# Second layer's MLP: 24 f tiles of M1 as seven half-size products per four tiles, M2's weight sums by accumulating transfers

## The chip, the cores and the metric

The kernel runs on one core of a Trainium2 chip. A core has five engines with instruction streams of their own: TensorE (PE; its weight loads are shown as PEld), VectorE (DVE), ScalarE (ACT), GpSimd (POOL) and SyncE (SP, which issues most transfers), and 16 DMA engines that move data between device memory and the on-chip memory. The metric is the device time of one execution in microseconds, and of several runs the median. The profile is one execution taken by the hardware profiler; its times are microseconds from the start of its span.

## The reference

A decoder of two layers on 512 tokens with D = 1024 and D_FF = 4096, in float32, cut to what matters here:

```
c_act = silu(c)
for i in range(2):
    sh1, sc1, g1, sh2, sc2, g2 = split(c_act @ ada_w[i] + ada_b[i], 6)
    h = rmsnorm(x, norm_mix_g[i]) * (1 + sc1) + sh1
    y = pool_mixer(h) if i == 0 else sgu_mixer(h)
    x = x + g1 * y
    h = rmsnorm(x, norm_mlp_g[i]) * (1 + sc2) + sh2
    x = x + g2 * (square(relu(h @ mlp_w1[i])) @ mlp_w2[i])
return rmsnorm(x, final_g)
```

`sgu_mixer` is a projection to 2048 columns with GELU, a layernorm of one half (v), a causal 128 x 128 mixing per head, a product with the other half (u) and a last projection, called M_o below. `mlp_w1` (1024 x 4096) is M1, `mlp_w2` (4096 x 1024) is M2.

## The kernel before

**Precision.** Each float32 operand of a large product is kept as two parts: hi, a rounded copy written by ScalarE, and lo, the difference written by VectorE (`split`, lines 135 to 140, for weights). A product is then three matmuls, lo x hi, hi x lo and hi x hi (`mm3`, lines 145 to 149). The partition size P is 128, KD = 8 tiles of D, NT = 4 tiles of tokens, S = 512 tokens. `hh` and `hl` hold the two parts of the normalised, transposed input.

**The MLP of a layer** is `mlp(i, first, extra, last, ending)` at line 506. M1 makes 32 f tiles of 128 columns each. An f tile takes eight steps over D, of three matmuls with 512 columns (`f_run`, line 544), and `put` (522) writes relu and then the square into `g` with ScalarE (532, 533). Eight f tiles form a chunk. M2 takes chunk 0, 1 and 2 as a 2 x 2 block product with seven half-size products instead of eight (`p_prep` 565, `p_run` 610, numbered 1, 5, 6, 3, 7, 2, 4 in the order in which they run; the pattern is that of Strassen and Winograd). Their operands are sums of blocks: VectorE adds blocks of M2's weights, 128 x 2048 each, in place (574, 580, 591, 599), and blocks of g (576, 582, 584, 588). The result is accumulated into `y` (632, 635), and in chunk 2 multiplied by the gate `gb` and added to x (the fold, 638 and 639). The last chunk is taken directly (`q_prep` 644, `q_run` 666), and the callback `last` finishes x.

**Order.** PE's instructions run in the order in which the program gives them. For the other engines a list scheduler sets the order, by priority and by when buffers come free. The units of the MLP (f tiles, products p, last products q) are listed in lines 678 to 689: after the first f tiles three f tiles of the next chunk, and from then on p and f in turn. Unit n + 2 is prepared (loaded and split) before unit n runs (694 to 697). Loads of weights use the pool `w4` (three buffers of 128 x 1024, shared with several smaller users), the split weights five pairs of buffers `wh`, `wl`, and blocks of M2 three buffers `b` of 1 MB.

**Extras.** Work for later that is spread over the units (698 to 700). In the second layer these are eight `ada_tile` (162; a load into a w4 buffer and a multiply-and-sum on VectorE), which make the last columns g2 of the modulation, then `spread_cols` (176), which spreads these columns over all partitions: eight GpSimd operations fill `dg` (line 180, a w4 buffer), two matmuls with a matrix of ones put it into PSUM (183), and ScalarE copies that into `gb` (184). The tenth extra, `load_fg` (873), loads the final norm's gain.

**Start of the second MLP.** In the M_o stage (838 to 853) `gated` (706) adds the mixer's result to x and collects the norm's sums; `power` on GpSimd (190) makes the inverse root. `normed(hf, ...)` (725) scales x, transposes it on PE (737) for one half of the tokens (256), applies the modulation into a tile `tt`, and makes hi and lo (745, 746). `first1` (855) runs f tiles 0 to 3 in two halves of 256 tokens: the first half of tiles 0, 1 and 2, then `normed` for the second half of the tokens, the first half of tile 3, and the second halves of the four.

The modulation's loads, the loads of x, M1 and M2 are issued on SP's queue.

Of the kernel before, what the change touches and what calls it, by code (L numbers as in the profile page):

```python
# [70 lines left out]
def decoder_kernel(ctx: ExitStack, tc: tile.TileContext, xtok, vecs, rows, fgrow, ada0, adag, ada1, pool_w, w1s, w1, w2, w2e, w_v, w_u, w_o, wsT, lnp, bs, out):  # L71
# [40 lines left out]
    x = big.tile([P, NT, D], F32, name="x")  # L112
    hh = big.tile([P, KD, S], F32R, name="hh")
    hl = big.tile([P, KD, S], F32R, name="hl")
    gb = big.tile([P, D], F32, name="gb")

# [83 lines left out]
    with (  # L200
# [29 lines left out]
        def squares(out, t, c, on):  # L230
            j = sq[:, 0 : c.stop - c.start]
            if on is A:
                A.activation(j, x[:, t, c], AF.Square, scale=D**-0.5, accum_out=out)
            else:
                V.scalar_tensor_tensor(j, x[:, t, c], 1.0 / D, x[:, t, c], ALU.mult, ALU.mult, accum_out=out)
# [39 lines left out]
        def load(name):  # L275
# [8 lines left out]
            if kind == "x":  # L284
                for t in range(NT):
                    nc.sync.dma_start(x[:, t], xtok[t])
            elif kind == "pw":
                c = slice(2 * d[0], 2 * d[0] + 2)
                nc.sync.dma_start(pw[:, c], pool_w[:, c])
            elif kind == "raw":  # L290
                sweep_load(d[0])
# [73 lines left out]
        def windows(g):  # L365

            for k in (2 * g, 2 * g + 1):
                po = pqs[k] = bank("pq")
                for t in range(NT):
                    n = P if t == NT - 1 else W  # L370
                    T.matmul(po[:, P * t : P * t + n], x[:, t, P * k : P * k + P], bandr[:, t, g, 0:n], start=(t == 0), stop=(t == NT - 1), skip_group_check=True)
# [18 lines left out]
        def add(g, h):  # L390
            c = slice(256 * g, 256 * g + 256)
            V.tensor_tensor(x[:, 2 * h : 2 * h + 2, c], x[:, 2 * h : 2 * h + 2, c], pos.pop((g, h)), ALU.add)  # L392
# [6 lines left out]
        def turn(g):  # L399

            for k in (2 * g, 2 * g + 1):
                pxs[k] = bank("px")
                for t in range(NT):
                    T.transpose(pxs[k][:, P * t : P * t + P], x[:, t, P * k : P * k + P], ident)
# [57 lines left out]
        def norm_hi(k):  # L462
            t = ht[k] = st2.tile([P, S], F32, name="ht", tag="ht")
            V.scalar_tensor_tensor(t, xf[:, k], scl[0][1][:, k : k + 1], rbs[0], ALU.mult, ALU.mult)
            A.activation(hh[:, k], t, AF.Identity, bias=mod(0, c_sh(1, k)))  # L465

        def norm_lo(k):
            V.scalar_tensor_tensor(hl[:, k], ht.pop(k), mod(0, c_sh(1, k)), f32(hh[:, k]), ALU.add, ALU.subtract)
# [22 lines left out]
        for k in range(KD):  # L491
# [11 lines left out]
            for f in range(SWEEP):  # L503
                mm3(sweep[f], cut(wk[k][1:], ALL, slice(P * f, P * f + P)), (hh[:, k], hl[:, k]), k == 0, k == KD - 1)


    def mlp(i, first, extra, last, ending):
# [3 lines left out]
        with (  # L511
# [6 lines left out]
            tc.tile_pool(name="yp", bufs=1) as yp,  # L518
# [3 lines left out]
            y = yp.tile([P, NT, D], F32, name="y")  # L522
            g = {}

            def put(f, po):
# [3 lines left out]
                if p == 0:  # L529
                    g[c, j] = gq.tile([P, 4, S], F32, name="g", tag="g")  # L530
                t = g[c, j][:, p]
                A.activation(t, po, AF.Relu)  # L532
                A.activation(t, t, AF.Square)  # L533
# [6 lines left out]
            def f_prep(u):  # L540
                c, f = u
                return split(raw4(w1[i, 8 * c + f]))

            def f_run(u, w):
# [3 lines left out]
                for k in range(KD):  # L548
                    mm3(po, cut(wv, ALL, k), (hh[:, k], hl[:, k]), k == 0, k == KD - 1)
# [3 lines left out]

            held = {}

            def b_of(c, r, n):
                t = w2p.tile([P, 4, S], F32, name="b", tag="b")
                nc.sync.dma_start(t, w2[i, c, r, n])
                return t

            def p_prep(u):
                c, m = u
                H = held
# [4 lines left out]
                if m == 1:  # L568
                    wb = H["b11"] = b_of(c, 0, 0)
                    a = quad(c, 0, 0)  # L570
                elif m == 5:
                    H["b12"] = b_of(c, 0, 1)
                    wb = H["t"] = H.pop("b11")
                    V.tensor_tensor(wb, H["b12"], wb, ALU.subtract)
                    a = H["s"] = s_tile("s")
                    V.tensor_tensor(a, quad(c, 1, 0), quad(c, 1, 1), ALU.add)
                elif m == 6:
                    H["b22"] = b_of(c, 1, 1)
                    wb = H["t"]
                    V.tensor_tensor(wb, H["b22"], wb, ALU.subtract)  # L580
                    a = H["s"]
                    V.tensor_tensor(a, a, quad(c, 0, 0), ALU.subtract)
                    H["u"] = s_tile("u")
                    V.tensor_tensor(H["u"], quad(c, 0, 0), quad(c, 1, 0), ALU.subtract)
                elif m == 3:
                    wb = H["b22"]
                    a = H["s"]
                    V.tensor_tensor(a, quad(c, 0, 1), a, ALU.subtract)
                elif m == 7:
                    wb = H.pop("b12")  # L590
                    V.tensor_tensor(wb, H.pop("b22"), wb, ALU.subtract)
                    a = H.pop("u")
                    H.pop("s")
                elif m == 2:
                    wb = H["b21"] = b_of(c, 1, 0)
                    a = quad(c, 0, 1)
                else:
                    wb = H.pop("t")
                    V.tensor_tensor(wb, H.pop("b21"), wb, ALU.subtract)
# [3 lines left out]
                A.activation(oh, a, AF.Copy)  # L603
                V.tensor_tensor(ol, a, f32(oh), ALU.subtract)
                w = [split(wb[:, 2 * q : 2 * q + 2].rearrange("p a b -> p (a b)")) for q in range(2)]
                return (oh, ol), w

            X, Z = {}, {}
# [4 lines left out]

            def p_run(u, ready):
# [3 lines left out]
                banks = X if m in (1, 6, 7, 4) else Z  # L618
                first, fin = m in (1, 5, 2), m in (4, 3, 2)
                if first:  # L620
                    for hf in halves:
                        banks[hf] = bank("pm", xz)
                for p in range(4):
                    wv = cut(w[p // 2], ALL, slice(S * (p % 2), S * (p % 2) + S))
                    for hf in halves:
                        mm3(banks[hf], cut(o, ALL, p, hf), wv, first and p == 0, fin and p == 3, skip_group_check=True)
                for hf in halves:
                    r, dh = TAKES[m]
                    t = 2 * hf + r
                    yt = y[:, t, S * dh : S * dh + S]  # L630
                    if (t, dh) in seen:
                        V.tensor_tensor(yt, yt, banks[hf], ALU.add)  # L632
                    else:
                        seen.add((t, dh))
                        A.activation(yt, banks[hf], AF.Copy)
                    if c == 2 and LAST.get(m) == (r, dh):

                        V.tensor_tensor(yt, yt, gb[:, S * dh : S * dh + S], ALU.mult)
                        V.tensor_tensor(x[:, t, S * dh : S * dh + S], x[:, t, S * dh : S * dh + S], yt, ALU.add)
# [4 lines left out]
            def q_prep(u):  # L644
# [8 lines left out]
                else:  # L653
                    o = w2p.tile([P, 2, KD, P], F32R, name="qo", tag="b")
                    oh, ol = o[:, 0], o[:, 1]
                for j in range(2):
                    a, k = g[3, j][:, :, tok[t]], slice(4 * j, 4 * j + 4)
                    A.activation(oh[:, k], a, AF.Copy)
                    V.tensor_tensor(ol[:, k], a, f32(oh[:, k]), ALU.subtract)
# [3 lines left out]
            kept = {}  # L663

            def q_run(u, o):
                dh, t = u

# [12 lines left out]
            for c in range(3):  # L680
                fs = [("f", (c + 1, f)) for f in range(8)]
                units += fs[0:3]
                fs = fs[3:]
                for m in (1, 5, 6, 3, 7, 2, 4):
                    units.append(("p", (c, m)))
                    if fs:
                        units.append(fs.pop(0))
            units += [("q", (dh, t)) for dh in range(2) for t in range(NT)]
            prep = {"f": f_prep, "p": p_prep, "q": q_prep}
            run = {"f": f_run, "p": p_run, "q": q_run}  # L690
# [3 lines left out]
            for n, (kind, u) in enumerate(units):  # L694
                for m in range(n, min(n + 3, len(units))):
# [5 lines left out]
                run[kind](u, ready[n])  # L701

# [3 lines left out]
    def gated(t, c0, n, src):  # L706
        tmp = sm.tile([P, S], F32, name="tmp", tag="tmp")[:, 0:n]
        xt = x[:, t, c0 : c0 + n]
# [16 lines left out]
    def normed(hf, i, n):  # L725

        xs = []
        for r in range(2):
            t = w4.tile([P, D], F32, name="xs", tag="w4")
            A.activation(t, x[:, 2 * hf + r], AF.Copy, scale=rms(2 * hf + r))  # L730
            xs.append(t)
        c = slice(256 * hf, 256 * hf + 256)
        for k in range(0, KD, 2):
# [4 lines left out]
            tt = sm.tile([P, 2, 256], F32, name="tt", tag="tmp")  # L738
# [240 lines left out]
```

## Time and profile before

| | |
|---|---|
| Median of 3 runs | 895.44 us (895.14 to 895.63) |
| The profiled execution | 895.87 us, of which the span is 894.2 us |
| Mean granted TensorE clock | 0.992 |
| Instructions on PE, DVE, ACT, POOL | 3980, 842, 609, 102 |

A row of a timeline gives the start, the busy time, the engine, the line of the program, the operation, its output and inputs by name and their sizes; in brackets is the engine's idle time just before it and what ended that. A row of a group gives the number of operations, their sum and the mean length in ns. `po`, `pm`, `px`, `pb` are PSUM tiles of the M1-like products, of M2, of the transposes and of `spread_cols`; `raw` is a loaded weight, `wh`, `wl` its two parts, `xs` the scaled x.

### The profile page before, as it was taken

What the parts mean: (1) busy time and instruction counts of PE and PEld (TensorE: products, weight loads), DVE (VectorE), ACT (ScalarE), POOL (GpSimd) and SP (SyncE); (2) the same over time, 40 slices, a digit from 0 to 9 for tenths busy, and PEclk for the clock granted to TensorE, in tenths of its full rate; (3) what the DMA queues carried; (4) which work ended last, traced back from release to release, by engine and by line L of the source; (5) the groups of instructions that cost most, each with busy time, mean ns of one, the idle gap of its engine ahead of it and who ended that gap; (6) DMA issues with size and microseconds to landing.
All of it is one profiled execution on the core that took longest, in us unless ns stands there. A gap on an engine that the chain in (4) does not pass through costs nothing.

```text
span 894.2 us, 10448 instructions
## 1 busy us (share of the span) xinstructions
PE 866.9 (97%) x3980; PEld 719.1 (80%) x3980; DVE 652.0 (73%) x842; ACT 419.8 (47%) x609; POOL 56.2 (6%) x102
## 2 busy tenths in 40 slices
PE   4979999999999999999999999999999999999996
PEld 2868888788888888888878888988887888888885
DVE  5879796779869888746798645657667666667954
ACT  3374755454444445347233336644545445445421
POOL 7000002000000000001310000000003000000000
PEclk9989999999999999999999999999999999999998
DMA  9939853563465442622657206622352134121312
GB/s 356 402 136 325 280 211 130 191 208 118 165 212 164 131 153 71 235 84 105 212 185 239 72 23 235 213 94 89 134 179 94 48 141 144 45 77 65 95 48 94
DMA packets 35475, 138.64 MB, mean 155 GB/s; under 512 B 3937, under 2 KB 4065, under 8 KB 32225
## 3 DMA queue, kind: packets, MB, share of 16 engines
q1 hardware_dynamic: 35282, 137.72, 44.5%
q8 instruction: 31, 0.51, 0.2%
q10 hardware_dynamic: 144, 0.26, 0.1%
q14 instruction: 18, 0.15, 0.0%
HBM read 135.87 MB, written 2.10 MB: 154 GB/s over the span
## 4 chain that ended last, share of the span: by engine, by line
PE 89%; DMA 5%; DVE 3%; ACT 2%; issue 0%; POOL 0%; SPq 0%; POOLq 0%; DVEq 0%; ACTq 0%
PE po L148 18%; PE po L149 18%; PE po L147 17%; PE pm L148 11%; PE pm L149 11%; PE pm L147 11%; DMA ada<-in_ada 1%; DMA wh<-in_adag 1%; DMA wl<-in_ada 1%; PE po L828 1%; DMA wh<-in_ada 1%; PE pb L183 1%; DVE ada L311 1%; DVE x L392 0%; ACT wh L138 0%
## 5 line engine op out<-in xcount | busy, mean ns | idle before, releaser
L147 PE MATMUL po<-hh,wl 128*128 128x512 f32 (+1 forms) x608 | 232.7, 383 | 2.5 <-ACT hh L465 2.4
L148 PE MATMUL po<-hl,wh 128*128 128x512 f32 (+1 forms) x608 | 231.2, 380 | 1.9 <-DVE hl L746 1.7
L149 PE MATMUL po<-hh,wh 128*128 128x512 f32 (+1 forms) x608 | 230.8, 380 | 0.0
L139 DVE TENSOR_TENSOR wl<-b,wh 128x1024 fp32r<-128x1024 f32 x84 | 102.5, 1222 | 70.6 <-ACT wh L138 70.6
L139 DVE TENSOR_TENSOR wl<-raw,wh 128x1024 fp32r<-128x1024 f32 x89 | 108.8, 1223 | 47.2 <-ACT wh L138 46.8
L148 PEld LDWEIGHTS po<-hl,wh 128*128 128x128 f32 x608 | 115.0, 189 | 24.8 <-DVE hl L746 2.1
L147 PEld LDWEIGHTS po<-hh,wl 128*128 128x128 f32 x608 | 115.1, 189 | 24.8 <-ACT hh L465 2.6
L149 PEld LDWEIGHTS po<-hh,wh 128*128 128x128 f32 x608 | 114.9, 189 | 21.4
L149 PE MATMUL pm<-wh,oh 128*128 128x512 f32 x336 | 130.7, 389 | 0.0
L147 PE MATMUL pm<-wh,ol 128*128 128x512 f32 x336 | 130.7, 389 | 0.0
L148 PE MATMUL pm<-wl,oh 128*128 128x512 f32 x336 | 130.7, 389 | 0.0
L138 ACT ACTIVATE wh<-raw 128x1024 fp32r<-128x1024 f32 x89 | 94.1, 1058 | 52.9 <-PE pm L149 34.0
L532 ACT ACTIVATE g<-po 128x512 f32<-128x512 f32 x64 | 38.0, 599 | 170.5 <-PE po L149 170.5
L138 ACT ACTIVATE wh<-b 128x1024 fp32r<-128x1024 f32 x84 | 88.5, 1053 | 15.1 <-PE pm L149 10.1
L169 DVE SCALAR_TENSOR_TENSOR ada<-ada,cb 128x1024 f32<-128x1024 f32 x56 | 68.1, 1219 | 20.0 <-DMA ada<-in_ada 20.0
L147 PEld LDWEIGHTS pm<-wh,ol 128*128 128x128 f32 x336 | 63.1, 188 | 13.1
L148 PEld LDWEIGHTS pm<-wl,oh 128*128 128x128 f32 x336 | 63.1, 188 | 13.1
L149 PEld LDWEIGHTS pm<-wh,oh 128*128 128x128 f32 x336 | 63.1, 188 | 13.1
L714 ACT ACTIVATE tmp<-x 128x512 f32<-128x512 f32 (+1 forms) x25 | 15.3, 613 | 64.5 <-DVE x L710 64.5
L632 DVE TENSOR_TENSOR y<-y,pm 128x512 f32<-128x512 f32 x68 | 43.4, 679 | 0.0
L533 ACT ACTIVATE g<-g 128x512 f32<-128x512 f32 x64 | 39.6, 624 | 0.0
L180 POOL TENSOR_SCALAR dg<-ident,mods 128x128 f32<-128x128 f32 x24 | 24.6, 1044 | 214.3 <-DVE wl L139 129.6
(161 smaller groups left out, 1155.2 us busy)
## 6 DMA issues: line engine op xcount, KB each, us to landing
ada<-in_ada SPq DMA_DIRECT2D x78, 512.0 KB, 4.1
raw<-in_w SPq DMA_DIRECT2D x57, 512.0 KB, 3.4
b<-in_w SPq DMA_DIRECT2D x24, 1024.0 KB, 4.8
raw<-in_w2e SPq DMA_DIRECT2D x16, 512.0 KB, 3.4
ur<-in_w_u SPq DMA_DIRECT2D x8, 512.0 KB, 4.9
raw<-in_w_v SPq DMA_DIRECT2D x8, 512.0 KB, 4.0
raw<-in_w_o SPq DMA_DIRECT2D x8, 512.0 KB, 4.2
wh<-in_ada SPq DMA_DIRECT2D x7, 512.0 KB, 9.8
```

The costliest lines, as they stand in the source:

```text
L138: A.activation(h, r, AF.Copy)
L139: V.tensor_tensor(l, r, f32(h), ALU.subtract)
L147: T.matmul(o, wl, mh, start=first, stop=False, **kw)
L148: T.matmul(o, wh, ml, start=False, stop=False, **kw)
L149: T.matmul(o, wh, mh, start=False, stop=last, **kw)
L169: V.scalar_tensor_tensor(r, r, 1.0, cb, ALU.mult, ALU.mult, accum_out=pmv[i, b][:, j : j + 1])
L180: G.tensor_scalar(dg[:, k], ident, cols[:, k : k + 1], None, ALU.mult)
L183: T.matmul(po, ones, dg[:, 4 * n : 4 * n + 4], start=True, stop=True)
L532: A.activation(t, po, AF.Relu)
L533: A.activation(t, t, AF.Square)
L632: V.tensor_tensor(yt, yt, banks[hf], ALU.add)
L714: A.activation(tmp, xt, AF.Square, scale=D**-0.5, accum_out=s[:, len(cs) : len(cs) + 1])
```

## The change

In the second layer only (the first layer gets the same code with its old shapes, and one sign convention is turned so that VectorE adds blocks of M2's weights where it subtracted them):

- The 24 f tiles of chunks 1 to 3 are made four at a time, as a 2 x 2 block product with seven half-size products (units "s": chunk c, group j of four f tiles, product m). The blocks are halves of D (512 rows), halves of the four f tiles (256 columns) and halves of the tokens (256). A product is eight steps of three matmuls with 256 columns. A block of weights is one 128 x 1024 buffer of w4; VectorE adds blocks in place and splits each sum. Four input sums (operands of products 5, 6, 3 and 7) are made once, from the float32 input `h32`, after f tiles 4 to 7, which run in two halves of 256 tokens now. Products 1, 5 and 6 copy their PSUM into g; 2, 3 and 7 add theirs to g on VectorE; relu and square follow.
- M2's weight sums of chunks 0 to 2 are no longer made by VectorE. GpSimd issues a transfer that adds the next block from device memory to the block in place (`b_add`), once the block's two parts have been made: the running sum `bt` gets the blocks for products 5, 6 and 4, another buffer gets the sum for product 7. There are two buffers `b` and one `bt` where three `b` were.
- x is two tiles of two token tiles each. After each `normed` of the second MLP its half is written to device memory (`spill`), and the space then holds the two parts of the operands of products 6 and 3. After the last product 4 of M1 x is loaded again (`reload`), followed by `load_fg`. The fold of chunks 0 to 2 moves from the p units to the q units.
- `h32` lies in the space of y, and of the mixer's v before that.
- The eight `ada_tile` of the extras move into the M_o stage, one after each `gated`. `spread_cols` is the only extra left, and so is issued with the first unit, before f tile 4 runs.
- A unit's preparation may be up to five weight buffers ahead in place of two units.
- The program is built with 8192 bytes of scratch memory for transfers whose descriptors GpSimd makes.

The core of the diff:

```diff
+            def a_sums(step):
+                def a(r, j):
+                    return h32[0][:, 4 * j : 4 * j + 4, 256 * r : 256 * r + 256]
...
+                if step == 0:
+                    sums_a.update({1: H(slice(0, 4), first), 2: H(slice(4, 8), first), 4: H(slice(4, 8), half)})
+                    shift(hx, GAP)
+                    minus(a(1, 1), a(1, 0), a(1, 1))
+                    m, o = 5, operand(hx, "hx")
+                elif step == 1:
+                    minus(a(1, 1), a(1, 1), a(0, 0))
+                    m, o = 6, operand(big, "x0")
+                elif step == 2:
+                    minus(a(0, 0), a(0, 0), a(1, 0))
+                    V.tensor_tensor(a(1, 1), a(1, 1), a(0, 1), ALU.add)
+                    m, o = 3, operand(big, "x1")
+                else:
+                    m, o = 7, H(slice(0, 4), half)
+                parts(o, a(0, 0) if m == 7 else a(1, 1))
...
+            def s_prep(u):
+                c, j, m = u
...
+                t = b(0, 0)
+                if m in CHAIN:
+                    V.tensor_tensor(t, t, b(*CHAIN[m]), ALU.add)
...
+                elif m == 7:
+                    wb = b(0, 1)
+                    V.tensor_tensor(wb, wb, b(1, 1), ALU.add)
...
+                w = split(wb)
...
+            def s_run(u, w):
...
+                for f in range(2):
+                    for k in range(4):
+                        mm3(po[:, f], cut(wv, ALL, k, slice(P * f, P * f + P)), cut(sums_a[m], ALL, k), start and f + k == 0, stop and f + k == 4, skip_group_check=True)
...
+            def b_add(t, c, r, n):
+                G.dma_start(t, w2[i, c, r, n], accum_op=ALU.add)
...
+                    nxt = {1: 5, 5: 6, 6: 4}.get(m)
+                    if nxt:
+                        b_add(wb, c, *CHAIN[nxt])
+                    if m == 3:
+                        b_add(B["b12"], c, 1, 1)
...
+                    fs, lead, step = [("s", (c + 1, j, m)) for j in range(2) for m in ORDER], 3, (2, 2, 2, 2, 2, 1, 0)
...
+                if i and kind == "f":
+                    a_sums(u[1] - 4)
+                if i and u == (3, 1, 4):
+                    reload()
...
+    def spill(h):
+        xd.append(dram.tile([P, 2, D], F32, name=f"xd{h}"))
+        G.dma_start(xd[h], x_[h])
+
+    def reload():
+        for h in range(2):
+            x_[h] = big.tile([P, 2, D], F32, name=f"x{h}", tag=f"x{h}")
+            G.dma_start(x_[h], xd[h])
+        load_fg()
...
-    ex = [lambda q=q: ada_tile(1, 40 + q, ada1[48 + q], get4) for q in range(8)]
-    ex += [lambda: spread_cols(mods[1][:, c_g(1, 0) : c_g(1, 0) + KD]), load_fg]
+    ex = [lambda: spread_cols(mods[1][:, c_g(1, 0) : c_g(1, 0) + KD])]
```

309 lines of the change are left out of this document (214 added, 95 removed).

## The prediction

> **What bounds the kernel now.** First the page: its span and busy times, then its chain of waits.
>
> ```profile
> span 894.2 us, 10448 instructions
> PE 866.9 (97%) x3980; PEld 719.1 (80%) x3980; DVE 652.0 (73%) x842; ACT 419.8 (47%) x609; POOL 56.2 (6%) x102
> PE 89%; DMA 5%; DVE 3%; ACT 2%; issue 0%; POOL 0%; SPq 0%; POOLq 0%; DVEq 0%; ACTq 0%
> ```
>
> TensorE is busy for 97% of the span and holds 89% of the chain, so time is won only by giving it less to do, and lost wherever it is made to wait. The changed part is the second layer's M1 and M2, from about 537 us on. The windows view (length, then PE, PEld, DVE, ACT, POOL busy, granted clock, DMA share, GB/s) shows it by stage:
>
> ```profile
> 537.00:574.00 37.00, 35.33 (x260) 33.19 (x259) 22.11 (x32) 24.71 (x38) 1.41 (x2) 1.00 0.64 228
> 596.00:664.00 68.00, 68.00 (x302) 56.33 (x301) 48.71 (x46) 35.79 (x46) 0.00 (x0) 1.00 0.35 116
> 664.00:730.00 66.00, 66.00 (x289) 53.94 (x288) 43.97 (x39) 31.87 (x40) 9.79 (x8) 1.00 0.25 88
> ```
>
> From 574 us TensorE never stops; VectorE is at 67 to 72%, ScalarE about half, the DMA engines a third. Before 574 us, where the normalised input is made, it loses about 1.7 us.
>
> **TensorE's work.** A busy matmul's length includes its drain, so I take the price from start to start in the timeline of PE: first the 512-column matmuls, 159 steps from the first to the second row, then the 256-column ones, 51 steps.
>
> ```profile
> 575.01 0.39 PE L147 MATMUL po<-hh,wl 128*128 128x512 f32 x1
> 611.05 0.39 PE L147 MATMUL po<-hh,wl 128*128 128x512 f32 x1
> ...
> 550.38 0.28 PE L149 MATMUL po<-hh,wh 128*128 128x256 f32 x1
> 556.49 0.28 PE L149 MATMUL po<-hh,wh 128*128 128x256 f32 x1
> ```
>
> That is 36.04/159 = 0.2267 us and 6.11/51 = 0.1198 us: half the columns cost 53%, with a new weight load for each. 24 f tiles now take 24 x 24 = 576 long matmuls, 130.6 us. Six groups of seven products, each 2 x 4 x 3 = 24 short matmuls, are 1008, or 120.8 us: **9.8 us less**. The four other f tiles after the first four now run in two halves: 192 short (23.0) for 96 long (21.8), **1.2 us more**.
>
> **The start of the layer.** Rows of the PE timeline, then DVE, then the DMA of the chain and the ScalarE operations behind it:
>
> ```profile
> 538.97 1.91 PE L737 MATMUL px<-ident,xs 128*128 128x128 f32 x16
> 550.15 0.39 PE L148 MATMUL po<-hl,wh 128*128 128x256 f32 x1 [1.31 <-DVE hl L746]
> 564.29 0.39 PE L148 MATMUL po<-hl,wh 128*128 128x256 f32 x1 [0.34 <-DVE hl L746]
> 573.50 0.28 PE L149 MATMUL po<-hh,wh 128*128 128x256 f32 x1
> 573.62 0.40 PE L147 MATMUL po<-hh,wl 128*128 128x512 f32 x1
> ...
> 540.84 3.93 DMA raw<-in_w
> 544.85 1.06 ACT wh L138
> ```
>
> In the built order of the changed kernel ScalarE makes all hi parts of the input (two pairs of tt and two of hh, about 4.2 us at 0.5 us each) before it splits any M1 weights, so both hl stalls should go. But eight ada loads now sit in the M_o stage and hold the w4 buffers; the first M1 weights can only load when the transposes that end near 540.6 release theirs: landing 544.7, ScalarE free at about 545.6, hi 546.7, lo 547.9. f tile 0 starts at 548.0 instead of 546.1. Then 3 tiles (8.6), transposes (1.7), one tile (2.9) and four second halves (11.5) end at 572.6, against 573.6: **1.0 us less**, with 0 and 2 as bounds (all gain eaten by late loads; first load no later than ScalarE's first split today). The eight multiplies of ada move to where VectorE is idle, and cost nothing while M_o runs; if it were late for the mixer's last two tiles, some 4 us of slack is in front of them. The spill of x is issued on POOL's queue ahead of the small power operations (line 190) that the transposes wait for. They have 1 to 3 us of slack.
>
> **A new wait.** spread_cols fills the buffer dg on POOL and multiplies it by ones (line 183) to make gb. It was the ninth extra of the layer, spread over many units; now it is the only one and stands in front of f tile 4 in PE's fixed order. In the built order dg gets the w4 buffer of f tile 7's weights, so POOL starts only after their lo part. The old trace has that subtraction, the three dg fills, pb, and for single fills the shortest, median and longest in ns:
>
> ```profile
> 572.52 1.22 DVE L139 TENSOR_TENSOR wl<-raw,wh 128x1024 fp32r<-128x1024 f32 x1 [1.66 <-ACT wh L138]
> ...
> 144.97 6.48 POOL L180 TENSOR_SCALAR dg<-ident,mods 128x128 f32<-128x128 f32 x8 [84.65 <-DVE ada L169]
> 421.78 8.34 POOL L180 TENSOR_SCALAR dg<-ident,mods 128x128 f32<-128x128 f32 x8 [12.98 <-DVE wl L139]
> 669.24 9.79 POOL L180 TENSOR_SCALAR dg<-ident,mods 128x128 f32<-128x128 f32 x8 [116.65 <-DVE wl L139]
> ...
> 682.62 1.72 PE pb L183 x4
> ...
> L180 POOL TENSOR_SCALAR dg<-ident,mods x24: 598/606/2673, 145.0 to 678.4; 128x128 f32<-128x128 f32 x24
> ```
>
> The subtraction waits for TensorE to leave f tile 2's second half, and ends 0.1 us after the last second half (573.74 against 573.62). So TensorE has nothing left when POOL begins. The fill takes 6.5 to 9.8 us, more the busier VectorE is; VectorE is busy for about 4.5 of the first 8 us here, so I take 8.0. The last half of pb (0.86) follows, then f tile 4: 0.2 + 8.0 + 0.2 + 0.9 = 9.3 us, less the 1.7 us that pb costs today: **7.5 us more** (6.0 to 9.3). The whole of M1 and M2 queues behind it on PE.
>
> After an idle stretch the clock is lower. The windows view around 62 us (length, PE busy, clock, DMA, GB/s), where TensorE stood still for 2.4 us, then the PE timeline:
>
> ```profile
> 63.00:63.50 0.50, 0.00 (x0) 1.00 0.74 115
> 63.50:64.00 0.50, 0.00 (x0) 0.64 0.92 352
> 70.00:70.50 0.50, 0.50 (x3) 0.54 1.04 359
> 70.50:71.00 0.50, 0.50 (x3) 1.00 0.80 297
> ...
> 64.40 0.79 PE L147 MATMUL po<-hh,wl 128*128 128x512 f32 x1 [2.43 <-ACT hh L465]
> ```
>
> The clock is at half from about 63.7 to 70.3, 5.9 us of it with matmuls. At half clock half the time is lost: 2.9 us. Below that, zero would need the idle to be too short, which 8 us is not. I take **2.3 us**, since half of pb runs inside the wait. The Trainium skill (TensorE: Matmul & The Clock Gate, Part 1) says that one idle window of about 3.4 us halves the clock and about 3.4 us of sustained work restores it. By that the loss is 1.7 us and the sum 0.6 us lower; the trace here shows a longer recovery.
>
> **Work that must stay hidden.** Groups of VectorE and ScalarE from 574 us on, and DMA issues with median time to landing:
>
> ```profile
> L139 DVE TENSOR_TENSOR wl<-raw,wh 128x1024 fp32r<-128x1024 f32 x32 | 39.1, 1222 | 20.4 <-ACT wh L138 20.4
> L632 DVE TENSOR_TENSOR y<-y,pm 128x512 f32<-128x512 f32 x34 | 21.7, 679 | 0.0
> L574 DVE TENSOR_TENSOR b<-b 128x2048 f32<-128x2048 f32 x3 | 6.9, 2284 | 0.0
> L138 ACT ACTIVATE wh<-raw 128x1024 fp32r<-128x1024 f32 x32 | 33.8, 1057 | 17.2 <-PE pm L149 15.5 <-DMA raw<-in_w2e 1.7
> ...
> raw<-in_w SPq DMA_DIRECT2D x57, 512.0 KB, 3.4
> b<-in_w SPq DMA_DIRECT2D x24, 1024.0 KB, 4.8
> ```
>
> Per chunk VectorE loses 4 sums of b (4 x 2.28) and 8 f splits (9.8), and gains 14 splits (17.1), 8 sums of M1 weights (9.8) and 6 half-wide updates of g from PSUM (4.1). In all: 21 + 14 lo parts of 1.222 (42.8), 14 y updates (9.5), 4 sums of g (4.9), 9.8 and 4.1, or 71 us beside 78 us of TensorE (336 x 0.1198 + 168 x 0.2267). It fits at 91%. ScalarE adds 6 more splits, 3 x 2 copies out of PSUM and stays near 65%. With five pairs of weight buffers each split has a window of four items, 11.2 us, for some 2.5 us of work; so I put 0.5 us for stalls here (0 to 4). The eight sums and splits of h (some 10 us of VectorE) lie beside the 23 us of f tiles 4 to 7. The folds of y into x, 16 operations of 0.68, only move from c = 2 into the last units. The reload of x leaves POOL's queue when the borrowed buffers are given up: x0's after product 6 of the last group, some 3 us before p7 of c = 2, and x1's after product 3. The first fold stands about 6 us after x0's in VectorE's order, against 4.8 us for a plain 1 MB; a late one holds VectorE some 3 us, while TensorE's next split has 9 us in hand. The final gain row loads later, in nobody's way. All these cost zero; without their cover, 1 to 5 us.
>
> **The sum.** -9.8 + 1.2 - 1.0 + 7.5 + 2.3 + 0.5 = +0.7 us. The profiled execution took 895.87 (894.2 of span and 1.67 around it), 0.43 above the median 895.44. So 896.6 for it, and **896.1 us** against the median.
>
> **The rivals.**
> 1. *Slower: the accumulating transfers.* M2's running sum bt is split, then POOL issues a transfer that adds the next block, and only then can it be split again. In a chunk the links 1 to 5 and 5 to 6 come in a row. bt is free (lo of p1's second half made) about 4.6 us before TensorE starts p1; p6 starts 22.4 us (two groups of a product and two halves, 11.2 us each) after p1. Each link takes L and 3.5 us (hi and lo of both halves behind it), less 1.1 as p6 needs only its first half: 2 x (L + 3.5) - 1.1 must fit into 27.0, so L up to 10.5 us is free. Beyond, three chunks lose 2 (L - 10.5) each. No row has L. A plain 1 MB lands in 4.8 us; one that reads twice as much takes 9.6, read, add and write in turn 14.4. I take 9.6 (twice the reading), just inside. At 12 us the loss is 9 and the time 905; at 14.4 it is 23 and 920. ScalarE and VectorE stand in order behind the late block.
> 2. *Faster: the wait at dg is short.* If POOL is not held off and the clock holds, 0.2 + 4.8 (eight of the median 606 ns) + 1.1 - 1.7 remain, 4.4 in place of 9.8: 890.7. Without any such wait, were dg filled early as at 669 us, 886. For it: TensorE's saving is sure. Against: the buffer's last user ends when PE's work does.
> 3. *Slower: VectorE in order.* At 91% busy, each wait for a ScalarE hi part (20.4 us in 32 splits, above) may come through to TensorE. If a quarter of 21 groups lose 1 us, 5 us: 901. Against: the 11.2 us windows.
>
> **How the numbers follow.** Forecast, the saving cancelled by the wait at dg: 0.43, with 893.0 to 899.4 from its bounds (terms 6.0 to 9.3, clock 1.7 to 2.9, start 0 to 2, stalls to 2). Rival 1: 0.18. Rival 2: 0.20. Rival 3: 0.19. A difference of 0.2%, 1.8 us, is about what a measurement tells from none. The forecast case divides into 0.05 faster, 0.32 same, 0.06 slower; with the rivals: faster 0.25, same 0.33, slower 0.42. The range, 888.5 to 905.0, leaves out the wait-free end of rival 2 and the upper end of rival 1, a tenth each.
>
> **What would show it.** Right: 256-column matmuls 0.12 us apart in all of M1; the first hl stalls gone and the second halves ending near 572.6; PE idle some 9 us before f tile 4, released by POOL's dg, then the clock at half for 3 to 6 us; no PE idle from there to the end of M2; accumulating transfers landing below 10.5 us. Wrong: dg filled before the second halves end; PE waiting for wl or wh of bt; VectorE's lo parts released late in the mixed units; a first load of M1 that lands after 546.

## The result, and the profile after

The changed kernel takes 899.04 us (median of 5 runs, 898.26 to 900.82), the kernel before in the same comparison 895.44 us (5 runs, 894.90 to 896.03). The ratio is 1.0043, with a 95% interval of 1.0028 to 1.0058: **slower by 0.4%**, about 3.6 us. The profiled execution took 898.52 us, 2.65 more than that of before; the accounts below are made between these two, since both have a trace.

First the page of the changed kernel (span, busy times, chain), then two of its windows, with the columns of the prediction:

```profile
span 896.8 us, 11663 instructions
PE 858.6 (96%) x4508; PEld 733.6 (82%) x4508; DVE 692.2 (77%) x898; ACT 450.0 (50%) x649; POOL 69.6 (8%) x118
PE 76%; DVE 10%; DMA 7%; ACT 3%; issue 2%; POOL 1%; SPq 0%; POOLq 0%; DVEq 0%; ACTq 0%
...
574.00:590.00 16.00, 8.29 (x42) 5.80 (x43) 9.43 (x8) 5.52 (x8) 8.39 (x8) 0.68 0.14 52
...
700.00:760.00 60.00, 60.00 (x392) 54.83 (x391) 51.26 (x53) 36.93 (x45) 2.58 (x3) 1.00 0.58 164
```

TensorE's busy time fell by 8.3 us, as M1 has less to do, but the span grew: one stretch, 574 to 590 us, holds half of it idle, at a mean clock of 0.68. From 700 to 760 us VectorE is busy for 85% of the time and ScalarE for 62%. What TensorE waited for from 545 us on (total, times, longest):

```profile
PE pb L198 <- POOL dg L195: 8.8, 2, 8.6
PE po L162 <- DVE wl L154: 1.4, 2, 1.2
PE pm L163 <- DVE wl L154: 0.6, 1, 0.6
PE po L162 <- ACT g L693: 0.5, 1, 0.5
PE pm L162 <- DVE ql L544: 0.4, 1, 0.4
```

The wait of 8.8 us is the one at `dg`. Its rows, in the timelines of PE and POOL and in the chain (the load of f tile 7's weights and the fill), and the clock around it in windows of 1 us:

```profile
572.62 0.28 PE L164 MATMUL po<-hb,wh 128*128 128x256 f32 x1
581.46 2.07 PE L198 MATMUL pb<-dg,ones 128*128 128x512 f32 x2 [8.56 <-POOL dg L195]
583.78 1.92 PE L198 MATMUL pb<-dg,ones 128*128 128x512 f32 x2 [0.24 <-POOL dg L195]
...
566.07 6.82 DMA raw<-in_w1f
575.34 8.40 POOL dg L195 x8
...
575.00:576.00 1.00, 0.00 (x0) 0.00 (x0) 1.00 (x2) 1.00 (x2) 0.66 (x1) 0.58 0.16 66
585.00:586.00 1.00, 1.00 (x5) 0.60 (x5) 0.85 (x1) 0.38 (x2) 0.00 (x0) 0.80 0.00 0
```

TensorE's last second half starts at 572.62 and f tile 4 at 584.87: 12.25 us, of which pb would take 1.7 at full clock. The weights of f tile 7 landed only at 572.9, their lo part was ready at 575.2, and only then did the buffer come free that `dg` fills.

Set against the kernel before, in the two profiled executions:

| Stretch | Before | After | Difference | Forecast |
|---|---|---|---|---|
| to the transposes of the second MLP | 538.97 | 539.68 | +0.7 | 0 |
| from there to the last second half | 34.53 | 32.94 | -1.6 | -1.0 |
| from there to f tile 4 (before: 0.12, and pb's 1.72 later) | 1.84 | 12.25 | +10.4 | +9.8 |
| f tile 4 to the first q unit, without pb | 266.6 | 258.3 | -8.4 | -8.6 and stalls |
| q units to the end | 52.2 | 53.7 | +1.5 | in the 0.5 of stalls |
| sum (the spans are 894.2 and 896.8) | | | +2.6 | +0.7 |

The differences are taken before rounding. The first row can't be told from chance: in the changed kernel and experiments 1, 2 and 5, which do the same work up to there, these transposes start between 538.0 and 540.2 us.

### The profile page after: what moved, and what is told of

The parts are those of the page before. It is cut to its first block, busy times and chain, and to the rows that moved or that the text cites. A ratio compares the mean times of both kernels' runs of the same rounds, so it can differ in the third digit from the quotient of the medians.

```text
span 896.8 us, 11663 instructions
## 1 busy us (share of the span) xinstructions
PE 858.6 (96%) x4508; PEld 733.6 (82%) x4508; DVE 692.2 (77%) x898; ACT 450.0 (50%) x649; POOL 69.6 (8%) x118
## 4 chain that ended last, share of the span: by engine, by line
PE 76%; DVE 10%; DMA 7%; ACT 3%; issue 2%; POOL 1%; SPq 0%; POOLq 0%; DVEq 0%; ACTq 0%
PE po L163 15%; PE po L164 15%; PE po L162 15%; PE pm L163 9%; PE pm L162 9%; PE pm L164 9%; DVE wl L154 4%; DMA raw<-in_w1f 2%; ACT wh L153 1%; DMA wl<-in_adag 1%; PE po L400 1%; DMA raw<-in_w1b 1%; PE pg L354 1%; DVE y L809 1%; POOL dg L195 1%
## 5 line engine op out<-in xcount | busy, mean ns | idle before, releaser
L162 PE MATMUL po<-hb,wl 128*128 128x512 f32 (+1 forms) x640 | 216.9, 339 | 2.9 <-ACT hb L480 1.7
L163 PE MATMUL po<-hb,wh 128*128 128x512 f32 (+1 forms) x640 | 214.6, 335 | 0.3 <-DVE hb L484 0.3
L164 PE MATMUL po<-hb,wh 128*128 128x512 f32 (+1 forms) x640 | 214.5, 335 | 0.0
L154 DVE TENSOR_TENSOR wl<-raw,wh 128x1024 fp32r<-128x1024 f32 x107 | 130.5, 1222 | 39.7 <-ACT wh L153 39.4
L153 ACT ACTIVATE wh<-raw 128x1024 fp32r<-128x1024 f32 x107 | 112.9, 1057 | 59.9 <-PE pm L164 29.0
L162 PEld LDWEIGHTS po<-hb,wl 128*128 128x128 f32 x640 | 120.6, 188 | 17.6 <-ACT hb L480 2.0
L163 PEld LDWEIGHTS po<-hb,wh 128*128 128x128 f32 x640 | 120.5, 188 | 14.6 <-DVE hb L484 0.8
L164 PEld LDWEIGHTS po<-hb,wh 128*128 128x128 f32 x640 | 120.6, 188 | 12.5
L154 DVE TENSOR_TENSOR wl<-b,wh 128x1024 fp32r<-128x1024 f32 x60 | 72.9, 1221 | 20.6 <-ACT wh L153 20.6
L153 ACT ACTIVATE wh<-b 128x1024 fp32r<-128x1024 f32 x60 | 63.2, 1055 | 13.7 <-DVE b L739 5.0
L154 DVE TENSOR_TENSOR wl<-bt,wh 128x1024 fp32r<-128x1024 f32 x24 | 28.9, 1222 | 18.8 <-ACT wh L153 18.8
L162 PE MATMUL po<-as,wl 128*128 128x256 f32 x144 | 40.5, 281 | 0.7 <-ACT g L693 0.5
```

The source lines that it names most:

```text
L153: A.activation(h, r, AF.Copy)
L154: V.tensor_tensor(l, r, f32(h), ALU.subtract)
L162: T.matmul(o, wl, mh, start=first, stop=False, **kw)
L163: T.matmul(o, wh, ml, start=False, stop=False, **kw)
L164: T.matmul(o, wh, mh, start=False, stop=last, **kw)
```

## The experiments

All kernels below start from the changed kernel; their ratios are to the kernel before on the same chip. The mixed units are the stretch in which products of M1 and of M2 take turns, after f tile 7 and up to the first q unit. Three questions: is the wait at `dg` the loss and can it go; what do the accumulating transfers cost; is VectorE's amount of work a bound.

**1. dg filled early.** One edit: the call of `spread_cols` moves from the extras to the end of `first1`, so that it takes its buffer before the loads of f tiles 4 to 7.

```diff
+        spread_cols(mods[1][:, c_g(1, 0) : c_g(1, 0) + KD])
         for f in range(n):
             put(f, pos[f])
...
-    ex = [lambda: spread_cols(mods[1][:, c_g(1, 0) : c_g(1, 0) + KD])]
+    ex = []
```

> spread_cols is called at the end of first1 in place of the layer's extras; everything else is the changed kernel. dg then takes a w4 buffer ahead of the loads for f tiles 4 to 7, and GpSimd can fill it while the four first f tiles run. Theory A (the wait at dg is the whole price): of the 12.3 us from the last second half to f tile 4 only pb's 1.7 us stay, so 10.6 us less, 888.4 us; up to 2 more if the weights of f tiles 4 and 5, which get two buffers in place of three, come late. Theory B (the wait lets VectorE, ScalarE and the loads get ahead, and without it the mixed units stall): TensorE waits for wl or wh after 600 us and the time stays above 893.

Measured: 891.18 us (888.02 to 892.49), ratio 0.9939 (0.9917 to 0.9960). The fill in the timeline of POOL, then what TensorE waited for from 540 us on:

```profile
558.17 6.94 POOL L195 TENSOR_SCALAR dg<-ident,mods 128x128 f32<-128x128 f32 x8 [6.00 <-DVE wl L154]
...
PE po L162 <- DVE wl L154: 3.9, 3, 1.5
PE pm L163 <- DVE wl L154: 1.4, 3, 0.8
PE po L162 <- ACT g L693: 1.1, 1, 1.1
```

The wait is gone and the clock never drops there. That the wait was the loss is shown. But of the 10.6 us not all are gained (0.0104 of the ratio is 9.3 us between medians; the profiled spans differ by 6.8): TensorE's other waits from 540 us on rise from 2.9 to 6.8 us. So both theories have a part: without the wait, stalls in the mixed units come through. That the wait had given VectorE and ScalarE a lead is the likely reason; it is not shown apart, and experiment 2 does not fit it alone.

**2. The same, with f tiles 4 to 7 in 512 columns** (`n = S` in `f_run`).

> As e1_early_fill, and f tiles 4 to 7 run in 512 columns instead of two halves. Theory A: the 192 matmuls of 0.1198 us become 96 of 0.2267, so 1.2 us less than e1: 887.2. Theory B: the sums of the operands are no later, but TensorE reaches the mixed units 1.2 us sooner, and as it waits for VectorE there, nothing is gained against e1.

Measured: 886.81 us (886.65 to 888.09), ratio 0.9900 (0.9883 to 0.9916), 0.4% below the first. TensorE's two largest waits:

```profile
PE po L162 <- DVE wl L154: 1.8, 3, 1.2
...
PE po L162 <- ACT g L693: 1.0, 1, 1.0
```

More was gained than the 1.2 us of the matmuls: its waits are also 3.1 us shorter (3.7 in all), so Theory B's "nothing is gained" is out. Why the stalls are fewer when TensorE arrives earlier, I did not isolate.

**3. Each accumulating transfer twice.**

```diff
-                G.dma_start(t, w2[i, c, r, n], accum_op=ALU.add)
+                for _ in range(2):
+                    G.dma_start(t, w2[i, c, r, n], accum_op=ALU.add)
```

> The changed kernel with each accumulating transfer issued twice, one after the other into the same block; M2's weight sums hold the added block twice, so this leaves the computation. The time to landing of a link goes from 8.1 us to about 17. By the threshold of the prediction (10.5 us free, two links per chunk) three chunks lose 2 x 6.5 us each: 39 us, 938. Rival: the links are further ahead of TensorE than I worked out (ScalarE waits for them 5.3 us at most and TensorE not at all), the loss is under 15 us: below 914.

Measured: 944.17 us, ratio 1.0535 (1.0513 to 1.0557). TensorE's waits, and the transfers from 600 to 840 us (count, size, median us to landing):

```profile
PE pm L162 <- ACT wh L153: 28.2, 6, 7.7
...
bt<-in_w POOLq DMA_DIRECT2D x16, 1024.0 KB, 8.3
raw<-in_w1b SPq DMA_DIRECT2D x20, 512.0 KB, 7.2
```

45 us more than the changed kernel, where the threshold gave 39: six waits, two in each chunk as counted, of up to 7.7 us, and a lower clock behind them (the mean granted clock is 0.965 against 0.986). The rival (under 15 us) falls: the links are close to their limit, and there are two a chunk. The size agrees partly by luck. The six waits are 28.2 us, 4.7 each where the threshold gave 6.5, and most of the rest is the lower clock, which the threshold's price leaves out. With links of about 17 us this puts the free length near 12 us (an estimate, 17 less 4.7), not at 10.5.

**4. M2's weight sums on VectorE again** (`by_dma = False`; the three buffers then are as in the kernel before).

> The changed kernel with M2's weight sums on VectorE again (three buffers b in place of two b and one bt, 12 sums of 2.28 us more, no accumulating transfers). VectorE is busy 172.6 of 186 us (85 to 87%) from 640 to 843 us and gets 27.4 us more in three chunks of 78. Theory A (each split has windows of some 11 us, so VectorE may be filled to the brim): it is 97% full, TensorE loses 0 to 8 us: 899 to 907. Theory B (VectorE's order of work comes through before it is full): more than 8 us, up to 20: 907 to 919.

Measured: 895.69 us (894.00 to 901.04, 8 runs), ratio 0.9996 (0.9977 to 1.0015). It is not slower than the changed kernel but 0.5% faster, outside what both theories allowed. Windows, and TensorE's waits:

```profile
760.00:843.00 83.00, 83.00 (x528) 75.31 (x527) 82.67 (x86) 53.36 (x67) 1.14 (x2) 1.00 0.30 108
...
PE pb L198 <- POOL dg L195: 9.3, 2, 9.1
PE po L162 <- DVE wl L154: 1.2, 1, 1.2
```

VectorE is busy 82.67 of 83 us, and TensorE does not wait once in the mixed units. So a full VectorE is no bound here; something that came with the accumulating transfers is (the transfers themselves, or the two `b` and one `bt` in place of three `b`).

**5. Early fill, 512 columns and sums on VectorE together.**

> e2_early_512 with M2's weight sums on VectorE as in e4_sums_on_vectore. In the changed kernel TensorE loses 2.6 us in the mixed units and after, in e2 4.2, in e4 0.4, though VectorE is busier there. Theory A (what comes through to TensorE is ScalarE and VectorE standing in order behind transfers, the accumulating ones above all, not VectorE's amount of work): the stalls go here too, 2 to 3 us below e2 on the same chip. Theory B (in e4 the 12 us wait at dg gave VectorE its lead, and it was full at the end, 82.7 of 83 us): without that lead VectorE's 27 us more come through, 3 to 12 us above e2.

Measured: 883.90 us (882.86 to 885.00), ratio 0.9853 (0.9827 to 0.9879), 0.5% below the second experiment. TensorE's waits from 540 us on are those of f tile 0 and of one q unit:

```profile
PE po L162 <- DVE wl L154: 1.2, 1, 1.2
PE pm L163 <- DVE wl L154: 0.2, 1, 0.2
```

Theory A holds: without the lead and with VectorE as full (57.4 of 60 us from 700 to 760 us, as in experiment 4), no stall is left.

**6. What of the accumulating transfers does it?** In the changed kernel ScalarE and VectorE waited for transfers from 574 to 845 us:

```profile
ACT wh L153 <- DMA bt<-in_w: 18.1, 5, 5.3
...
DVE raw L653 <- DMA raw<-in_w1b: 16.9, 5, 5.0
```

They stand behind the block that is being added to, and behind M1's blocks, which land in 4.8 us there (655 to 840 us) and in 3.4 in experiment 5. Either the order of the work (the chain of split, add, split) is the cause, or the traffic. Two kernels on top of experiment 5 add traffic without a chain. The first writes both parts of a product's operand to device memory, 1 MB, at the places of the accumulating transfers:

```diff
+                if i == 1 and m in (1, 5, 6, 3):
+                    G.dma_start(scratch[0][:, 0], oh)
+                    G.dma_start(scratch[0][:, 1], ol)
```

> e5_early_512_vectore (M2's sums on VectorE, no stalls), and GpSimd issues 12 times a write of an operand's two parts (1 MB) to device memory, where the changed kernel issues its accumulating transfers; nothing waits for them but the operand's buffer two products later. Theory A (in the changed kernel ScalarE and VectorE stand in order behind the block that is being added): no stall, 883.9 within 1 us. Theory B (it is the traffic: loads of M1's blocks land in 4.8 to 6.7 us there and in 3.4 in e5, and VectorE waits 16.9 us for them against 0.6): these loads get longer here too, and 1 to 3 us of stalls come back, 885 to 887.

The second adds them instead of writing them, in chunks 1 and 2:

```diff
+                            G.dma_start(t, f32(o), accum_op=ALU.add)
```

> As e9_traffic_without_chain, and in chunks 1 and 2 these 16 transfers of 512 KB add to device memory instead of writing it; again nothing waits for them but the operand's buffer. In e9 the writes took 1.8% of the DMA engines' time per MB, in the changed kernel the accumulating transfers 3.3%. Theory A (standing in order behind the block): no stall, 883.9 within 1 us. Theory B (adding transfers hold the DMA engines about twice as long per byte and so delay the loads of M1's blocks): from 655 us on the loads land in 4.5 us or more instead of 3.4, VectorE waits for them, and TensorE loses 1 to 3 us.

Measured: 883.88 us, ratio 0.9859 (0.9844 to 0.9874), and 883.31 us, ratio 0.9854 (0.9838 to 0.9871); neither differs from experiment 5 (0.9853), and TensorE's waits are the same two. The transfers of the second from 655 to 840 us, and then those of the changed kernel in the same stretch (the queue of GpSimd's transfers with its packets, MB and share of the 16 engines; then count, size, time to landing):

```profile
q0 software_dynamic: 2592, 10.49, 30.5%
raw<-in_w1b SPq DMA_DIRECT2D x14, 512.0 KB, 4.7
idle<-oh POOLq DMA_DIRECT2D x8, 512.0 KB, 5.2
```

```profile
q0 software_dynamic: 1440, 10.49, 27.1%
raw<-in_w1b SPq DMA_DIRECT2D x16, 512.0 KB, 4.8
bt<-in_w POOLq DMA_DIRECT2D x6, 1024.0 KB, 8.1
```

The traffic is as heavy, and M1's blocks land as late in the median (4.7 us), yet TensorE waits for nothing more than in experiment 5. So traffic of this amount costs nothing, and the chain is left: engines that work in order stand behind a block that is not there yet, and carry that delay to the next weights. In the changed kernel one such case can be followed, from ScalarE's wait for `bt` to TensorE:

```profile
791.97 1.06 ACT L153 ACTIVATE wh<-bt 128x1024 fp32r<-128x1024 f32 x1 [3.03 <-DMA bt<-in_w]
...
804.19 0.36 PE L162 MATMUL po<-as,wl 128*128 128x256 f32 x1 [0.20 <-DVE wl L154]
```

Between them VectorE waits 2.6 us for ScalarE (793.06) and ScalarE 3.5 us for VectorE (800.52). That the chain is the whole cause is not shown. The latest of M1's blocks are later in the changed kernel: of those issued in this stretch, 5 of 14 take 6.9 to 8.1 us there and 1 of 12 takes more than 5.6 us in the second kernel, where VectorE waits 1.6 us for them in place of 16.9. Nor were the two `b` and one `bt` tried apart. And the stalls of the q units stand behind loads of M2's last weights (ScalarE waits 2.7 us at 842.21 for `raw<-in_w2e`), whose link to the chain was not followed.

**7. The ada tiles back among the extras**, with `spread_cols` behind them, as in the kernel before.

> The changed kernel with the eight ada tiles back among the second layer's extras, spread_cols behind them (about unit 20 instead of the first); nothing else. Theory A: the M1 weights for f tile 0 come 1.2 us sooner, dg is filled while TensorE has work and 10.6 us of wait and low clock go; VectorE's 10 us of ada work lie between 574 and 680 us beside 87% of load: together about 11 us below the changed kernel, at most 3 of them lost to stalls. Rival: ada tiles and dg take one of the three w4 buffers in turn, so that blocks of M1 load late: TensorE waits more than 5 us in the mixed units and the gain is under 6 us.

Measured: 909.76 us (907.93 to 910.46), ratio 1.0142 (1.0118 to 1.0167): both theories missed it. TensorE's waits:

```profile
PE pb L198 <- POOL dg L195: 9.3, 2, 9.1
PE po L162 <- DVE wl L154: 7.3, 3, 4.6
```

The wait at `dg` does not go away at unit 20; it only moves (POOL starts the fill at 667.72, released by a lo part as before). The likely reason: the w4 buffers are taken by blocks that are prepared several units ahead, so that at both places `dg` gets a buffer only when TensorE is about to need it. In the kernel before, half of the units did not use this pool. And as the rival said, TensorE waits more in the mixed units: 7.3 us for wl against 1.4. That the ada tiles in this pool delay M1's blocks is the rival's reason, and was not tested alone.

**8. M1 in f tiles again**, with M2 by accumulating transfers. The sums of the input go with the products, and the reload of x is no longer held back by borrowed space.

> The changed kernel with M1's chunks 1 to 3 as f tiles of 512 columns again, as in the kernel before; M2 by accumulating transfers, spill, reload and the early spread_cols stay. By the prediction's prices 1008 x 0.1198 us of products become 576 x 0.2267, 9.8 us more; the stalls of the mixed units (1 us) may go: 8 to 10 us above the changed kernel. If the products' saving is partly lost elsewhere, for example in stalls behind VectorE, it is less than 7.

Measured: 902.94 us (902.39 to 906.57), ratio 1.0086 (1.0058 to 1.0114), only 3.9 us above the changed kernel in the profiled spans (900.7 against 896.8). The trace divides this: from f tile 4 to the first q unit 270.3 us against 258.3, so M1 as products saves 12.0 us there. (Part of that is this kernel's own: its M1 matmuls of 512 columns take 0.2294 us from start to start, against 0.2267 in the kernel before, 1.6 us over 576.) But in this kernel `dg` falls on the buffer of another tile, and its fill starts before the second halves end and finds VectorE idle:

```profile
572.87 4.67 POOL L195 TENSOR_SCALAR dg<-ident,mods 128x128 f32<-128x128 f32 x8 [8.61 <-DVE wl L154]
...
572.80:577.60 4.80, 3.65 (x27) 2.82 (x25) 0.00 (x0) 1.21 (x2) 4.67 (x8) 1.00 0.87 271
```

TensorE waits 1.1 us in place of 8.8. The second halves end 2.7 us later (f tile 0 waits 3.3 us in place of 1.2), and the q units take 1.4 less. So the low difference is not a saving lost in the mixed units, as the expectation had it; the edit moved the wait too, which I had not seen.

**9. Folds one by one** (on top of experiment 5: one fold before each q unit, not four before the first), run twice:

> As e5_early_512_vectore, with one fold of y into x ahead of each last product instead of four ahead of the first. In the changed kernel VectorE has 8 fold operations (5.4 us) between the splits that the last products need, and TensorE loses 1.2 us there against 0.4 before. If the folds are the cause, 0.5 to 1 us below e5; if not, the same as e5 within 0.3.

> e8_folds_one_by_one again, as the measure for e10 on the same chip: 883.0, ratio 0.985 to the kernel before.

Measured: 883.04 us (882.85 to 883.68), ratio 0.9849 (0.9827 to 0.9870), and 882.95 us (882.60 to 883.63), ratio 0.9849 (0.9833 to 0.9866). The difference to experiment 5 is within the noise, and in experiment 5, with four folds before the first q unit, the waits of the q units were gone already: the folds alone are not their cause. Whether they add to them in the changed kernel was not tried. These are the fastest kernels of the study, **1.5% below the kernel before** and about 1.9% below the changed one.

**10. The ada tiles ahead of M_o** (on top of experiment 9).

> e8_folds_one_by_one with the eight ada tiles ahead of M_o, in the stage of the u tiles behind the 16 that are there (one is left for M_o). In all kernels with them in M_o TensorE waits 1.2 us for the lo part of f tile 0's weights, whose load starts when the transposes release its buffer. Theory A (an ada tile holds the third w4 buffer until then): f tile 0 starts without a wait, 1.2 us below e8 on the same chip. Rival: the two xs tiles and the last M_o weights hold the buffers in any case, no change, or up to 3 us more if the u stage, with 24 ada tiles in place of 16, becomes slower.

Measured: 884.74 us, ratio 0.9868 (0.9853 to 0.9883), 1.8 us above its measure. TensorE's waits from 500 us on:

```profile
PE po L162 <- DVE wl L154: 1.2, 1, 1.2
PE po L162 <- DVE gtl L1052: 1.2, 1, 1.2
```

A wait in M_o is added, and f tile 0 waits 1.2 us as before. But the load of its weights did move: here are its issue, then ScalarE's last hi parts of the input and its first splits of M1's weights.

```profile
525.39 0.33 SPq L141 DMA_DIRECT2D raw<-in_w1f  x1
...
545.66 1.16 ACT L543 ACTIVATE hb<-h 128x512 fp32r<-128x512 f32 x2
546.70 2.95 ACT L153 ACTIVATE wh<-raw 128x1024 fp32r<-128x1024 f32 x3
```

It is issued 15 us earlier than in experiment 9 (540.51) and lands 3.2 us later, long before it is used. So the ada tiles in M_o did hold its buffer, as Theory A had it, and yet nothing is won: ScalarE splits the weights only after the hi parts of the input. Its order, not the load, sets the start of f tile 0. Another place for these splits in that order was not tried.

## Why the prediction was right, and where it was off

The forecast of 896.1 us, "the saving cancelled by the wait at dg", had its own bounds at 893.0 and 899.4; 899.04 is at their upper end. (The lower and the upper ends of its terms add up to 892.5 and 901.0, so these bounds were drawn too narrow.) The mechanism is what the trace shows, and experiments 1, 2 and 5 take it away. I gave "within 0.2%" 0.33 and "slower" 0.42; it is slower, by 0.4%, 3.6 us where the sum had 0.7. Step by step:

- **TensorE's saving.** Forecast -9.8 + 1.2 = -8.6; found -8.4 from f tile 4 to the q units, but by terms that I had wrong, so that the agreement is partly luck. The price of the short matmul, 0.1198 us, was taken from before. In the changed kernel the first and the last of 57 steps are

```profile
550.03 0.28 PE L164 MATMUL po<-hb,wh 128*128 128x256 f32 x1
556.74 0.28 PE L164 MATMUL po<-hb,wh 128*128 128x256 f32 x1
```

  6.71/57 = 0.1177 us. With it 1008 products take 118.6, 12.0 less than the f tiles, and the halves cost 0.8. On the other side the long matmuls of M2, 23 steps in each kernel (changed, then before), became slower:

```profile
650.02 0.40 PE L162 MATMUL pm<-wh,ol 128*128 128x512 f32 x1
655.27 0.39 PE L164 MATMUL pm<-wh,oh 128*128 128x512 f32 x1
```

```profile
655.25 0.39 PE L147 MATMUL pm<-wh,ol 128*128 128x512 f32 x1
660.47 0.39 PE L149 MATMUL pm<-wh,oh 128*128 128x512 f32 x1
```

  5.25/23 = 0.2283 against 5.22/23 = 0.2270: 0.7 us over 504. Stalls of about 1 us and the last 0.7 us of pb, which fall behind f tile 4's recorded start, make up most of the rest.
- **The start of the layer.** f tile 0 was forecast at 548.0 and started at 548.27 in an execution that was 0.7 us late already; the second halves ended at 572.7, forecast 572.6. Against before it is -1.6, not -1.0. The prediction had the splits behind ScalarE's hi parts, and so it is (experiment 10).
- **The wait at dg.** The fill took 8.4 us for my 8.0, beside 4.56 us of VectorE's work in 8.5 (I had 4.5 in 8); with VectorE idle it took 4.67 us (experiment 8). The Trainium skill (SBUF — State Buffer, Who interferes with whom) has a VectorE instruction with two inputs in SBUF contend with a GpSimd instruction that reads SBUF; the two fills agree with that. VectorE's busy time alone does not set it: in experiment 1 the fill took 6.94 us, with VectorE busy for 5.54 of them. What failed is "ends 0.1 us after the last second half": this subtraction ended 2.3 us after TensorE had stopped. f tile 7's load was issued only when an earlier f tile's weights, which had taken 7.1 us to land beside the spill and two 1 MB loads, were split; and it took 6.8 us itself, beside M2's first accumulating transfer, which was issued at 563.01 and took 8.9:

```profile
563.01 0.93 POOL L716 DMA_DIRECT2D b<-in_w  x1 [10.54 <-DMA raw<-in_w1f]
```

  That load is not the whole cause. Experiment 4 has no such transfer, and these are its load and its subtraction:

```profile
566.16 3.35 DMA raw<-in_w1f
...
572.99 1.22 DVE L154 TENSOR_TENSOR wl<-raw,wh 128x1024 fp32r<-128x1024 f32 x1
```

  The weights are there at 569.51, and still the subtraction ends at 574.21, 2.3 us after TensorE had stopped (571.91). ScalarE and VectorE are busy with the sums of the input, which the prediction had put beside f tiles 4 to 7 at no cost; five of their eight operations on VectorE ran ahead of this subtraction in the changed kernel.
- **The clock.** Half speed from 575.2 to 585.4. TensorE started again at 581.46, and the first half of pb, which needs only four of the eight fills, ran beside the rest of the fill at no cost. The second half took about 1.75 us in place of 0.86: 0.9 lost, forecast 2.3. This gave back part of what the late subtraction cost: wait and clock come to 11.1 us for 9.8, with pb's last 0.7 that the table has in its next row. The clock came back 3.9 us after TensorE started again, sooner than in the stretch at 62 us from which I took the price (5.9). The Trainium skill's 3.4 us (TensorE: Matmul & The Clock Gate, Part 1) are nearer, and would have given 1.7 (an estimate).
- **Stalls, forecast 0.5 (0 to 4).** Counted from start to start of TensorE's matmuls, about 1 us in the mixed units and 1.2 more in the q units: 2.2 together, over four times the term. Its cause is neither the folds alone (experiments 5 and 9) nor VectorE's 91% (experiments 4 and 5). It came with the accumulating transfers: engines in order behind blocks that were still being added to, in the main (experiments 4 to 6). Rival 1 has this in its last sentence, but at no cost below its threshold.
- **Rival 1**, the accumulating transfers: L is 8.1 us, not 9.6, below the 10.5 that I gave as free, and its price beyond was tested at twice the length: 45 us for 39, of which the waits are 28 (experiment 3). But "free below the threshold" was wrong: even there the transfers cost TensorE some 2 us.
- **Rival 2**, a short wait: did not occur. Without any wait I gave 886. Experiment 1, which takes the wait away and nothing else, has 891, as stalls take part of its place; experiment 2 reaches 887 with a second edit.
- **Rival 3**, VectorE in order at 91%: the amount is refuted, 99% is harmless when what VectorE needs is there in time (experiment 4). The order of the work counts, by another path than I had put it.

## What to carry to other kernels

A small step that fills a shared buffer and is waited for in TensorE's fixed order can cost its full length once the buffers run several units ahead: see whose last use frees its buffer, and take the buffer before the deep prefetch begins. Moving sums from a full engine to accumulating transfers gains nothing if that engine has its operands in time, and costs something if engines that work in order then stand behind the transfer. And before a load is moved forward, see whether it is the load that its user waits for: experiment 10 brought one 15 us forward and won nothing. When a wait of 10 us is taken out of a tuned order, look for stalls that it had covered.

## What the runs showed that I had not expected

- An accumulating transfer of 1 MB lands in 7.8 to 9.5 us (655 to 840 us of the changed kernel), against 4.8 for a plain one (two plain loads of `bt` that ran beside one took 7.2 and 9.1), and adding takes about twice the DMA engines' time per byte: in experiment 6 GpSimd's queue moved 10.49 MB in the same number of packets, at 30.5% of 185 us where it added and at 15.5% where it wrote, both with the reload of x.
- VectorE at 82.67 of 83 us beside a TensorE that never waits.
- The step of the 256-column matmul is 0.1177 us in place of 0.1198, and that of M2's 512-column matmul 0.2283 in place of 0.2270, between 574 and 843 us only: in the first layer of the changed kernel it is 0.2265 to 0.2270. The changed kernel has its moving operands of the short matmuls 64 bytes off the old alignment (the `GAP` of 16 words), which may be the reason for the first; for the second I have none. Neither was tried alone. In experiment 8, with the same offset, M1's matmuls of 512 columns take 0.2294: the offset, if it is that, does not make every shape faster.
